# Output projection by halves of the tokens, with squares summed and weights cut on GpSimd

## The chip, the cores and the metric

The kernel runs on one core of a Trainium2 chip. The metric is the device time of one execution in microseconds (us). The kernel before took 2391.41 us, the median of 3 runs (2388.33 to 2393.7). A core has five engines that run their own instruction streams: TensorE (PE, matrix products; its weight loads are shown as PEld), VectorE (DVE), ScalarE (ACT), GpSimd (POOL) and SyncE (SP, which here issues the transfers).

## The reference, cut to what matters

Two blocks run one after the other, each with two layers, on 512 tokens of width 1024, in float32. The first block (three kinds of attention with gates) is not touched. A layer of the second block computes:

```python
h = rms_norm(x, norm1) * (1.0 + scale1) + shift1
proj = h @ w_in
y_pool = pool_mixer(u, pool_w, pool_scale)             # 512 wide
y_nsa = nsa_mixer(q, k, v, gates, ...)                 # 8 heads of 64, two softmax branches each
mix = concatenate([y_pool, y_nsa]) @ w_out
x = x + gate1 * mix
h2 = rms_norm(x, norm2) * (1.0 + scale2) + shift2      # needs the sum of squares over all 1024 of x
x = x + gate2 * (square(relu(h2 @ w_ff1)) @ w_ff2)
```

## The kernel before, in words

Everything is kept transposed: a tile has 128 of the 1024 channels as partitions and the 512 tokens as columns, so x is eight tiles `x(0)` to `x(7)`. Products are exact to float32 by splitting both sides into a high and a low part: `mm3` makes three products (high x high, high x low, low x high) for each pair of a 128x128 weight block and a token tile.

Weights come as units of 128x1024 (`unit`, line 430). SyncE loads a unit into `wraw`, ScalarE casts its high part into `wH` (line 452), VectorE subtracts to get the low part `wL` (line 453, here called a cut). In the second block there are three buffers of `wH` and of `wL`.

In the attention part of a layer (`main2`, line 1416) a main stream of projections is woven with side streams: `nsa` (line 1734) handles eight heads with two branches each, in two overlapping stages. The first stage makes scores on TensorE, masked rows on VectorE (line 710), exponentials on ScalarE (line 711), the reciprocal and the gate as `rsum` on VectorE (lines 1759 and 1760), and scales the probabilities, the first two of four token tiles on GpSimd (line 1764) and the others on VectorE (line 1766). The second stage transposes on TensorE, splits on ScalarE and VectorE (lines 419 and 420) and multiplies with the values. Other projections fill TensorE meanwhile: after the values (`values`, line 1485) come four units for the pooled channels, four units `o2` of the output projection for the pooled half of the mix, and two units `o2h` for heads 0 to 3 (two 128-row blocks of the mix).

The last part of the output projection takes heads 4 to 7 (`yn` blocks 2 and 3) with two units `("o2h", l, 1, 0)` and `("o2h", l, 1, 1)`, each for four output tiles. The first goes through `quad_unit` (line 550): each output over all 512 tokens in a PSUM bank of its own. The second goes through `in_halves` (line 478): first all four outputs for tokens 0 to 255, then all four for tokens 256 to 511. For each output that is done, `use2` (line 1521) adds it to x on VectorE (line 1507) and calls `stat_step` (line 647): ScalarE squares, VectorE adds the square to the running sum `ssq` (lines 657 and 661, shown as `keep`); the last output's square is not added but goes into the column sums as a second tile.

`turn` (line 500) carries this into the next projection. It drains the first half of the `in_halves` work, begins `stat_half` (line 663) of the first half, which it sets into the second half of the products after the yields numbered in `SLOTS = (1, 3)`, then drains the rest. A `stat_half` makes column sums on TensorE, the scale on VectorE (line 574), the power -1/2 on GpSimd (line 578), a broadcast by four short products on TensorE and a copy to `rbc` on ScalarE (line 678). Then `h2` (line 1341) makes the new h of that half, eight tiles, with two VectorE instructions (lines 1347 and 1349) and one of ScalarE (line 1348) each. The first three units of the next projection are done by halves too (`first`).

The order of instructions on each engine is set when the kernel is built: a planner simulates the program by program order, by priorities (`unit` asks for an early place) and by readiness; `issue_after` ties an instruction behind another. On the chip each engine runs its list in that order.

Of the kernel before, what the change touches and what calls it, by code (L numbers as in the profile page):

```python
# [11 lines left out]
AF = mybir.ActivationFunctionType  # L12
ALU = mybir.AluOpType
# [208 lines left out]
def fbits(ap):  # L222
    return ap.bitcast(F32)
# [53 lines left out]
class Builder:  # L277
    def __init__(self, ctx, tc, dram):
        self.tc = tc
        self.nc = tc.nc  # L280
        self.dram = dram
        self.sb = ctx.enter_context(tc.tile_pool(name="sb"))
        self.ps = ctx.enter_context(tc.tile_pool(name="ps", space=bass.MemoryType.PSUM))
        self.units = []
        self.uid = 0
        self.stream = "m"
        self.acc = "acc"
        self.block = "1"
        self.flags = set()
        self.squares = []  # L290
        self.queue = {}
        self.norms = 0
        self.background = iter(())
        self.bgrate = self.bgc = 0.0
# [135 lines left out]
    def unit(self, spec, whole=False):  # L430
        nc = self.nc
        i = len(self.units)
        self.units.append(spec)
        with self.tc.high_priority(offset=3000):
            raw = self.t((P, 1024), "wraw", 2)
            if i in self.queue:
                with self.tc.issue_after(self.queue[i].ins):
                    self.load = nc.sync.dma_start(raw, self.dram["wp"][i])
            else:
                self.load = nc.sync.dma_start(raw, self.dram["wp"][i])  # L440
            if whole:
                return raw
            if spec[0] == "gates":

                h = self.t((P, 8, 2, 32), "wH", 4, F32R)
                r = raw[:, 0:256].rearrange("p (k c) -> p k c", k=KT)
                self.cut_h = nc.scalar.copy(h[:, :, 0, :], r)
                self.cut = nc.vector.tensor_sub(h[:, :, 1, :], r, fbits(h[:, :, 0, :]))
                return h.rearrange("p k w c -> p (k w c)"), None
            h = self.t((P, 1024), "wH", 4, F32R)  # L450
            l = self.t((P, 1024), "wL", 4, F32R)
            self.cut_h = nc.scalar.copy(h, raw)  # L452
            self.cut = nc.vector.tensor_sub(l, raw, fbits(h))  # L453
        return h, l

    def after_unit(self, out, in_):
# [18 lines left out]
            self.products(ps, h, l, k, src.h(k), src.l(k), k == 0, k == KT - 1)  # L475
        return ps

    def in_halves(self, jobs, src, use, k0=0):


        made = []

        def emit(half):
            ts = slice(256 * half, 256 * half + 256)
            for i, (spec, outs) in enumerate(jobs):
                if half == 0:
                    made.append((self.unit(spec), [self.psum("acc") for _ in outs]))
                (h, l), ps = made[i]
                nk = KT // len(outs)
                for a, m in enumerate(outs):  # L490
                    for k in range(nk):
                        mm = self.products(ps[a][:, ts], h, l, a * nk + k, src.h(k0 + k, ts), src.l(k0 + k, ts), k == 0, k == nk - 1)
                        if k == nk - 1:
                            use(m, ps[a], ts)
                        if (a * nk + k) % 4 == 3:
                            yield mm

        return emit
# [147 lines left out]

    def stat_step(self, ssq, x, k, ts=None):
        nc = self.nc
        if k == 0:
            nc.scalar.activation(ssq, x, AF.Square)  # L650
        elif ts is not None:
            sq = self.tmp()[:, ts]
            nc.scalar.activation(sq, x[:, ts], AF.Square)
            if k == KT - 1:
                self.squares.append(sq)
            else:
                nc.vector.tensor_tensor(ssq[:, ts], ssq[:, ts], sq, ALU.add)
        else:
            sq = self.tmp()
            nc.scalar.activation(sq, x, AF.Square)  # L660
            nc.vector.tensor_tensor(ssq, ssq, sq, ALU.add)
# [689 lines left out]
    def block2(self, l, x, par, mt, ssq, emit, out):  # L1351

        nc = self.nc
        self.flags.clear()
        drain(self.background)
        us = {"u": [u_s("w_in_2", l, P * g) for g in range(4)], "k": [u_s("w_in_2", l, 1024 + 384 * s) for s in range(2)],
              "g": [("gates", l)]}
        us = [x for p in ORDER if p in us for x in us[p]][:NFIRST]
        hs, first = self.turn(emit, ssq, x, mt[:, 48:56], mt[:, 0:8], us)
        S = dict(l=l, par=dict(par, **self.params2_rest(l)), hs=hs, x=x, mt=mt, first=first)  # L1360

        def chain():
            yield from self.nsa_prep(S)
            yield from self.nsa(S)

        self.weave(self.main2(S), [["s", chain(), RATE2], ["c", self.compressed(S), RATEC], ["p", self.pool(S), RATEP]])
        us = [u_s("w_ff1_2", l, P * m) for m in range(NFIRST)]
        hs, first = self.turn(S["emit"], S["ssq"], x, mt[:, 56:64], mt[:, 24:32], us)

        f = {}  # L1370
        nxt = None
        if out is None:
            nxt = self.start_mod(l + 1)

        def ff1(q):
            f[q] = self.hl(KT)
            for m in range(KT):
                ps = first[m] if q == 0 and m < NFIRST else self.proj_s(u_s("w_ff1_2", l, 1024 * q + P * m), hs)
                r = self.tmp()
                nc.scalar.activation(r, ps, AF.Relu)  # L1380
                r2 = self.tmp()
                nc.vector.scalar_tensor_tensor(r2, ps, 0.0, r, ALU.max, ALU.mult)
                self.split(f[q].h(m), f[q].l(m), r2)
                if q > 0:
                    self.bg_step()

        s2 = self.new_ssq()

        def add(m, ps, ts=slice(None)):
            nc.vector.scalar_tensor_tensor(x(m)[:, ts], ps[:, ts], mt[:, 40 + m:41 + m], x(m)[:, ts], ALU.mult, ALU.add)  # L1390

        def add_last(m, ps, ts=None):
            add(m, ps, ts or slice(None))
            if out is None:
                self.stat_step(s2, x(m), m, ts)
            else:
                nc.sync.dma_start(out[:, m, ts or slice(None)], x(m)[:, ts or slice(None)])

        def ff2(q):
            use = add_last if q == 3 else add  # L1400
            n = KT - NLAST if q == 3 else KT
            for m in range(n):
                use(m, self.proj_s(("f2", l, q, m), f[q]))
                self.bg_step()
            return self.in_halves([(("f2", l, q, m), [m]) for m in range(n, KT)], f[q], use)

        ff1(0)
        ff1(1)
        ff2(0)
        ff1(2)  # L1410
        ff2(1)
        ff1(3)
        ff2(2)
        return s2, ff2(3), nxt

    def main2(self, S):
        nc, hs, l, x, mt = self.nc, S["hs"], S["l"], S["x"], S["mt"]
# [67 lines left out]
        def values():  # L1485

            ps = yield from self.proj_m([("kvs", l, i) for i in range(4)], hs)
            kw = S["kraw"] = self.b4((P, TT, 256))
            V = S["V"] = self.b4((P, 2, TT, P), F32R)
            W = S["W"] = self.b4((P, 2, TT, P), F32R)  # L1490
            for tt in range(TT):
                with self.soon():
                    nc.scalar.copy(kw[:, tt, :], ps[tt][:, 0:256])
                    src = ps[tt][:, 256:512].rearrange("p (b g d) -> p b g d", b=2, g=2)
                    for b, t in enumerate((V, W)):
                        self.split(t[:, :, tt, 0:64], t[:, :, tt, 64:128], src[:, b])
            self.flag("kv")
            self.rate["s"] = RATE3
            self.acc = "accn"

        parts = {"u": pooled, "k": windows, "g": gates, "q": queries, "w": hidden, "v": values}
        for p in ORDER:
# [11 lines left out]
        for mq in range(2):  # L1514
            for i, _ in enumerate(self.quad_unit(("o2h", l, 0, mq), S["yn"], 0, 4 * mq, use)):
                if i % 2:
                    yield
        yield "yn"
        ssq = S["ssq"] = self.new_ssq()

        def use2(m, ps, ts=None):
            use(m, ps, ts or slice(None))
            self.stat_step(ssq, x(m), m, ts)

        yield from self.quad_unit(("o2h", l, 1, 0), S["yn"], 2, 0, use2)
        S["emit"] = self.in_halves([(("o2h", l, 1, 1), [4, 5, 6, 7])], S["yn"], use2, 2)

    def pool(self, S):
        nc, l, par = self.nc, S["l"], S["par"]
# [372 lines left out]

NFIRST = 3
NLAST = 2
NLASTP = 2

SLOTS = (1, 3)

# [63 lines left out]
```

## Time and profile before

| | |
|---|---|
| median of 3 runs | 2391.41 us |
| the profiled execution, its own time | 2391.33 us |
| its span | 2389.5 us |
| TensorE (PE) busy | 2342.3 us, 98% |
| VectorE (DVE) busy | 1640.2 us, 69% |
| ScalarE (ACT) busy | 1048.7 us, 44% |
| GpSimd (POOL) busy | 264.3 us, 11% |
| chain that ended last | PE 93%, DVE 5%, ACT 1%, issue 1% |

The page divides the span into 40 slices of about 60 us; each digit is the busy share in tenths:

```profile
PE   8999999999999999999999989999999998999999
DVE  5679975567588987656579886666647988644342
POOL 0011010000001001000055310000005531000000
```

The second block begins at about slice 19. Its two layers show as the two places at which GpSimd is busy (slices 20 to 23 and 30 to 33). An engine's busy time says nothing of what bounds a stretch: which wait ends last there does. A busy TensorE counts products that are running, at either of the two levels of its clock (2.4 GHz, shown as 1.00, and 1.2 GHz, shown as 0.50; a value between them is a mean over the stretch).

### The profile page before, as it was taken

The numbers are of one execution on the slowest core, as the hardware profiler recorded it, in microseconds if no ns is written. First come the engines' busy times: TensorE is split into PE (matmuls) and PEld (weight loads), VectorE is DVE, ScalarE is ACT, GpSimd is POOL, SyncE is SP. The second block draws the span as 40 slices with busy tenths as digits, with TensorE's granted clock in tenths as the row PEclk, the third lists the DMA queues.
The fourth block names the chain that finished last, engine by engine and source line by source line (L and its number), as shares of the span: only waits on it lengthen the run. The fifth ranks groups of instructions, "written<-read, shape, count | busy, mean of one in ns | idle before, by whom it ended". The sixth has DMA issues, their size and how long they took to land.

```text
span 2389.5 us, 31476 instructions
## 1 busy us (share of the span) xinstructions
PE 2342.3 (98%) x11684; PEld 1973.3 (83%) x11684; DVE 1640.2 (69%) x3410; ACT 1048.7 (44%) x1930; POOL 264.3 (11%) x254
## 2 busy tenths in 40 slices
PE   8999999999999999999999989999999998999999
PEld 7888888888888888888888778888888876888888
DVE  5679975567588987656579886666647988644342
ACT  6455543434446554343246654332324665433231
POOL 0011010000001001000055310000005531000000
PEclk9999999999999999999999999999999999999999
DMA  5222222245543222225332013555523211223222
GB/s 173 88 80 71 80 80 97 82 156 205 182 159 115 71 80 80 97 88 172 126 102 80 27 37 104 193 194 194 193 97 105 68 35 37 80 94 100 98 93 84
DMA packets 87851, 256.62 MB, mean 107 GB/s; under 512 B 9745, under 2 KB 10769, under 8 KB 87697
## 3 DMA queue, kind: packets, MB, share of 16 engines
q1 hardware_dynamic: 87552, 254.45, 31.9%
q8 instruction: 92, 1.51, 0.3%
q14 instruction: 63, 0.51, 0.1%
q10 hardware_dynamic: 144, 0.15, 0.0%
HBM read 250.37 MB, written 4.19 MB: 107 GB/s over the span
## 4 chain that ended last, share of the span: by engine, by line
PE 93%; DVE 5%; ACT 1%; issue 1%; DMA 0%; POOL 0%; DVEq 0%; ACTq 0%; POOLq 0%
PE acc L406 78%; PE M L406 5%; PE accn L406 4%; PE S L406 3%; PE M L415 3%; DVE p L420 1%; DVE p L710 1%; DVE b L1507 1%; DVE wL L453 1%; ACT p L419 0%; DVE p L1766 0%; ACT p L711 0%; DVE tmp_s L1794 0%; DMA wraw<-wp_in 0%; ACT tmp_s L1792 0%
## 5 line engine op out<-in xcount | busy, mean ns | idle before, releaser
L406 PE MATMUL acc<-h,wH 128*128 128x512 f32 (+2 forms) x2944 | 872.6, 380 | 9.5 <-ACT h L423 7.3
L452 ACT CAST wH<-wraw 128x1024 fp32r<-128x1024 f32 x358 | 375.2, 1051 | 656.8 <-PE acc L406 400.0
L406 PEld LDWEIGHTS acc<-h,wH 128*128 128x128 f32 (+1 forms) x2944 | 537.4, 189 | 106.1 <-ACT h L423 7.3
L453 DVE TENSOR_TENSOR wL<-wraw,wH 128x1024 fp32r<-128x1024 f32 x358 | 437.5, 1223 | 164.9 <-ACT wH L452 156.9
L406 PE MATMUL acc<-h,wL 128*128 128x512 f32 (+1 forms) x1440 | 546.2, 380 | 0.0
L406 PE MATMUL acc<-b,wH 128*128 128x512 f32 (+1 forms) x1696 | 503.9, 374 | 0.0
L406 PEld LDWEIGHTS acc<-b,wH 128*128 128x128 f32 x1696 | 311.8, 189 | 56.3
L406 PEld LDWEIGHTS acc<-h,wL 128*128 128x128 f32 x1440 | 272.7, 190 | 49.6
L406 PE MATMUL acc<-wH,h 128*128 128x512 f32 (+1 forms) x1024 | 310.0, 380 | 0.0
L406 PE MATMUL acc<-b,wL 128*128 128x512 f32 (+1 forms) x784 | 291.5, 372 | 0.0
L406 PEld LDWEIGHTS acc<-wH,h 128*128 128x128 f32 x1024 | 187.2, 188 | 33.7
L406 PE MATMUL acc<-wL,h 128*128 128x512 f32 (+1 forms) x512 | 194.7, 380 | 0.0
L1390 DVE SCALAR_TENSOR_TENSOR b<-acc,keep,b 128x512 f32<-128x512 f32 (+1 forms) x68 | 48.9, 720 | 183.9 <-PE acc L406 183.5
L406 PEld LDWEIGHTS acc<-b,wL 128*128 128x128 f32 x784 | 147.9, 189 | 25.4
L711 ACT ACTIVATE p<-p,nb 128x128 f32<-128x128 f32 x192 | 107.9, 564 | 77.7 <-DVE nb L710 76.7
L1325 DVE SCALAR_TENSOR_TENSOR keep<-keep 128x512 f32<-128x512 f32 x192 | 126.0, 686 | 11.1 <-DMA keep<-w_mod_in 10.9
L578 POOL TENSOR_TENSOR sm_bs<-sm_as,keep 128x4 f32<-128x4 f32 (+1 forms) x48 | 65.7, 1376 | 413.4 <-DVE sm_as L574 374.1
L406 PEld LDWEIGHTS acc<-wL,h 128*128 128x128 f32 x512 | 96.5, 188 | 16.2
L406 PE MATMUL S<-b,b 128*128 128x128 f32 (+3 forms) x480 | 108.9, 338 | 0.1
L710 DVE CUSTOM_DVE_ANT_0 p<-S,keep 128x128 f32<-128x128 f32 x192 | 101.3, 542 | 4.9 <-PE S L406 3.6
L415 PE MATMUL M<-keep,p 128*128 128x128 f32 x608 | 97.4, 275 | 2.7 <-DVE tmp_s L1794 1.0
L406 PE MATMUL M<-p,b 128*128 128x256 f32 (+3 forms) x352 | 81.7, 323 | 10.3 <-DVE p L420 9.0
(294 smaller groups left out, 2898.8 us busy)
## 6 DMA issues: line engine op xcount, KB each, us to landing
wraw<-wp_in SPq DMA_DIRECT2D x364, 512.0 KB, 3.5
keep<-w_mod_in SPq DMA_DIRECT2D x192, 256.0 KB, 3.6
b<-x_in SPq DMA_DIRECT2D x8, 256.0 KB, 6.3
g<-x_in SPq DMA_DIRECT2D x8, 256.0 KB, 4.4
x_spill<-tmp_m SPq DMA_DIRECT2D x8, 256.0 KB, 3.9
g<-x_spill SPq DMA_DIRECT2D x8, 256.0 KB, 3.8
out<-b SPq DMA_DIRECT2D x6, 256.0 KB, 2.0
keep<-parq_in SPq DMA_DIRECT2D x2, 384.0 KB, 6.9
```

Source lines behind the costliest of these rows:

```text
L406: return self.nc.tensor.matmul(out, l, r, start=start, stop=stop)
L415: self.nc.tensor.transpose(out, in_, self.ident[:n, :n])
L420: return self.nc.vector.tensor_sub(l, src, fbits(h))
L452: self.cut_h = nc.scalar.copy(h, raw)
L453: self.cut = nc.vector.tensor_sub(l, raw, fbits(h))
L578: self.pow = nc.gpsimd.tensor_tensor(r[:p, :n], m[:p, :n], self.mhalf[:p, :n], ALU.pow)
L710: nc.vector.tensor_tensor_reduce(p, s, mask, nscale, 3e38, ALU.add, ALU.min, accum_out=nb)
L711: nc.scalar.activation(p, p, AF.Exp, bias=nb, scale=-1.0, accum_out=accum)
L1325: nc.vector.scalar_tensor_tensor(w, w, 1.0, crow[:, T * k:T * k + T], ALU.mult, ALU.mult, accum_out=ms[:, 2 * f + k:2 * f + k + 1])
L1390: nc.vector.scalar_tensor_tensor(x(m)[:, ts], ps[:, ts], mt[:, 40 + m:41 + m], x(m)[:, ts], ALU.mult, ALU.add)
L1507: nc.vector.scalar_tensor_tensor(x(m)[:, ts], ps[:, ts], mt[:, 16 + m:17 + m], x(m)[:, ts], ALU.mult, ALU.add)
```

## The change

Three things change in the second block, in both layers. The second part of the heads' output projection goes wholly through `in_halves`: all eight outputs for tokens 0 to 255, then all eight for tokens 256 to 511, two outputs sharing a PSUM bank (`shared`), so that all 96 products have 256 columns. The additions of squares in that part run on GpSimd (`adder`). And from the end of the value projection to the last heads the cuts of weight units run on GpSimd (`cutter`): ten units per layer, four for the pooled channels, four `o2`, two `o2h` for heads 0 to 3. The square of output 0 goes straight into its half of `ssq`.

```diff
     def unit(self, spec, whole=False):
...
-            self.cut = nc.vector.tensor_sub(l, raw, fbits(h))
+            self.cut = self.cutter.tensor_tensor(l, raw, fbits(h), ALU.subtract)
...
-    def in_halves(self, jobs, src, use, k0=0):
+    def in_halves(self, jobs, src, use, k0=0, shared=False):
...
-                    made.append((self.unit(spec), [self.psum("acc") for _ in outs]))
+                    made.append((self.unit(spec), None if shared else [self.psum("acc") for _ in outs]))
                 (h, l), ps = made[i]
                 nk = KT // len(outs)
                 for a, m in enumerate(outs):
+                    if shared:
+                        if m % 2 == 0:
+                            bank = self.psum("acc")
+                        o = bank[:, 256 * (m % 2):256 * (m % 2) + 256]
+                    else:
+                        o = ps[a][:, ts]
                     for k in range(nk):
-                        mm = self.products(ps[a][:, ts], h, l, a * nk + k, src.h(k0 + k, ts), src.l(k0 + k, ts), k == 0, k == nk - 1)
+                        mm = self.products(o, h, l, a * nk + k, src.h(k0 + k, ts), src.l(k0 + k, ts), k == 0, k == nk - 1)
                         if k == nk - 1:
-                            use(m, ps[a], ts)
+                            use(m, o if shared else ps[a], ts)
...
     def stat_step(self, ssq, x, k, ts=None):
         nc = self.nc
-        if k == 0:
+        if k == 0 and ts is not None:
+            nc.scalar.activation(ssq[:, ts], x[:, ts], AF.Square)
+        elif k == 0:
             nc.scalar.activation(ssq, x, AF.Square)
...
-                nc.vector.tensor_tensor(ssq[:, ts], ssq[:, ts], sq, ALU.add)
+                self.adder.tensor_tensor(ssq[:, ts], ssq[:, ts], sq, ALU.add)
...
         hs, first = self.turn(S["emit"], S["ssq"], x, mt[:, 56:64], mt[:, 24:32], us)
+        self.adder = nc.vector
...
             self.acc = "accn"
+            self.cutter = nc.gpsimd
...
+        self.cutter = nc.vector
         yield "yn"
         ssq = S["ssq"] = self.new_ssq()

-        def use2(m, ps, ts=None):
-            use(m, ps, ts or slice(None))
+        def use2(m, ps, ts):
+
+            nc.vector.scalar_tensor_tensor(x(m)[:, ts], ps, mt[:, 16 + m:17 + m], x(m)[:, ts], ALU.mult, ALU.add)
             self.stat_step(ssq, x(m), m, ts)

-        yield from self.quad_unit(("o2h", l, 1, 0), S["yn"], 2, 0, use2)
-        S["emit"] = self.in_halves([(("o2h", l, 1, 1), [4, 5, 6, 7])], S["yn"], use2, 2)
+        self.adder = nc.gpsimd
+        S["emit"] = self.in_halves([(("o2h", l, 1, mq), [4 * mq + i for i in range(4)]) for mq in range(2)],
+                                  S["yn"], use2, 2, True)
```

## Rows read from the trace of the kernel before

**Rows 1.** Busy time by stage: window, PE, PEld, DVE, ACT, POOL, PE clock, DMA.
```profile
1272.00:1410.00 138.00, 130.43 (x722) 107.85 (x721) 126.06 (x346) 89.73 (x236) 50.91 (x62) 1.00 0.12 39
1410.00:1420.00 10.00, 6.72 (x45) 5.35 (x42) 5.37 (x13) 4.16 (x10) 2.14 (x2) 1.00 0.16 53
1420.00:1430.10 10.10, 10.10 (x54) 8.94 (x54) 7.69 (x14) 3.67 (x6) 0.00 (x0) 0.83 0.01 2
1430.10:1440.70 10.60, 4.71 (x22) 4.41 (x20) 6.90 (x16) 4.12 (x11) 0.72 (x1) 0.67 0.31 99
1440.70:1450.00 9.30, 9.29 (x65) 9.29 (x66) 9.12 (x25) 5.74 (x14) 0.86 (x1) 0.82 0.00 0
1872.00:2003.50 131.50, 123.99 (x691) 102.53 (x690) 119.36 (x328) 87.43 (x229) 44.65 (x53) 1.00 0.11 37
```

**Rows 2.** Waits of PE, 1420 to 1441: us in total, times, longest.
```profile
PE M L406 <- DVE keep L657: 4.6, 1, 4.6
```

**Rows 3.** Timeline of DVE, 1422 to 1437: start, us, instruction.
```profile
1431.42 1.22 DVE L453 TENSOR_TENSOR wL<-wraw,wH 128x1024 fp32r<-128x1024 f32 x1
...
1433.27 2.88 DVE L657 TENSOR_TENSOR keep<-keep,tmp_m 128x256 f32<-128x256 f32 x6
```

**Rows 4.** Timeline of all engines, from the last heads to the next projection.
```profile
1419.98 1.12 PE L406 MATMUL accn<-b,wH 128*128 128x512 f32 x2 [2.04 <-ACT b L419]
...
1434.82 0.58 PE L406 MATMUL M<-keep 128*128 128x1 f32 x2 [4.59 <-DVE keep L657]
...
1437.13 0.72 POOL L578 TENSOR_TENSOR sm_bm<-sm_am,keep 128x2 f32<-128x2 f32 x1 [24.99 <-DVE sm_am L574]
...
1437.90 1.22 PE L406 MATMUL M<-keep,sm_bm 128*128 128x128 f32 x4 [1.22 <-POOL sm_bm L578]
...
1439.16 0.37 ACT L678 COPY keep<-M 128x256 f32<-128x256 f32 x1 [5.82 <-PE M L406]
...
1440.71 0.58 PE L406 MATMUL acc<-h,wH 128*128 128x256 f32 x1
```

**Rows 5.** Timeline of PE, 1455 to 1462, at full clock.
```profile
1456.00 0.40 PE L406 MATMUL acc<-h,wH 128*128 128x256 f32 x2
...
1456.36 0.40 PE L406 MATMUL acc<-h,wH 128*128 128x256 f32 x2
...
1460.66 0.63 PE L406 MATMUL acc<-h,wH 128*128 128x512 f32 x2
```

**Rows 6.** Groups of PE, 1420 to 1430.1: count, busy us, mean ns, idle before.
```profile
L406 PE MATMUL accn<-b,wH 128*128 128x512 f32 x12 | 4.9, 476 | 2.0 <-ACT b L419 2.0
```

**Rows 7.** Groups of DVE, 1420.5 to 1440.7.
```profile
L1507 DVE SCALAR_TENSOR_TENSOR b<-acc,keep,b 128x256 f32<-128x256 f32 x8 | 3.5, 477 | 0.0
...
L657 DVE TENSOR_TENSOR keep<-keep,tmp_m 128x256 f32<-128x256 f32 x6 | 2.5, 425 | 0.5
...
L661 DVE TENSOR_TENSOR keep<-keep,tmp_m 128x512 f32<-128x512 f32 x3 | 2.1, 686 | 0.0
```

**Rows 8.** Groups of ACT, 1420 to 1440.7.
```profile
L653 ACT ACTIVATE tmp_m<-b 128x256 f32<-128x256 f32 x8 | 2.6, 402 | 0.0
```

**Rows 9.** Groups of POOL, whole span, shapes kept apart.
```profile
L1546 POOL TENSOR_TENSOR tmp_p<-b 128x511 f32<-128x511 f32 x8 | 8.7, 1081 | 0.0
...
L1605 POOL TENSOR_TENSOR b<-keep 128x256 f32<-128x256 f32 x4 | 4.0, 998 | 0.0
```

**Rows 10.** Groups of DVE, 1272 to 1410.
```profile
L453 DVE TENSOR_TENSOR wL<-wraw,wH 128x1024 fp32r<-128x1024 f32 x11 | 13.4, 1217 | 0.0
```

**Rows 11.** Timeline of POOL, 1305 to 1310.
```profile
1306.05 0.19 POOL L1545 COPY tmp_p<-tmp_p 128x2 f32<-128x2 f32 x1
...
1307.29 1.11 POOL L1545 COPY tmp_p<-tmp_p 128x4 f32<-128x4 f32 x1
```

**Rows 12.** Timeline of DVE, 1306.5 to 1310.
```profile
1307.14 1.22 DVE L453 TENSOR_TENSOR wL<-wraw,wH 128x1024 fp32r<-128x1024 f32 x1
...
1308.94 1.00 DVE L420 TENSOR_TENSOR tmp_p<-tmp_p,tmp_p 128x512 fp32r<-128x512 f32 x1
```

More of the change, by code (lines that the diff above doesn't have):

```diff
@@ L284, in __init__ @@
         self.units = []
+        self.adder = self.nc.vector
+        self.cutter = self.nc.vector
         self.uid = 0
@@ L1904 @@
 NLAST = 2
-NLASTP = 2
 SLOTS = (1, 3)
```

## The prediction

> **What bounds the kernel now.** I read the page first: TensorE is busy for 98% of the span and the chain that ended last is TensorE for 93%, so a change pays only where TensorE stands still or runs at the lower clock. The row of slices shows two weak places, one in each layer of the second block, so I then read the busy time by stages [rows 1]. From the end of the value projection to the last heads (1272 to 1410 us) TensorE is busy 130.43 of 138 us and VectorE 126.06: both nearly full, with 7.6 us of idle TensorE. The same stretch of the second layer has 123.99 of 131.5, 7.5 us. The tail of the last two heads (1410 to 1420) leaves 3.3 us idle. Then comes the place that the change rebuilds, the turn from the output projection to the feed-forward part: in 1430.1 to 1440.7 TensorE shows 4.71 us in 10.6, nothing of it long matmuls, and the granted clock is 0.67.
>
> The waits of that stretch name one cause: 4.6 us for `keep` of line 657, the running sum of squares on VectorE [rows 2]; 1.2 us for GpSimd's power come behind it [rows 4]. In the second layer the same two waits are 4.6 and 1.1 us. Why VectorE is late is seen in its timeline [rows 3]: when TensorE has ended its products at 1430.1, VectorE still has a cut of weights before it (1431.42) and, from 1433.27 on, six additions of 256 columns. Only then can the chain of the norm start [rows 4]: column sums at 1434.82, power at 1437.13, broadcast at 1437.90, copy, scale and shift, and the first product of the next projection at 1440.71. From the high half of the last heads (1419.98) to there it is 20.7 us (20.6 in the second layer, from 2013.55 to 2034.17), while TensorE's products in it are worth about 9.
>
> Reason for the order: before, the first half of the tokens is not complete until the quad unit over all 512 tokens and its additions are done, and after the second half's four outputs no product is left to hide the norm of the first half. So the chain of the norm lies open in full.
>
> **The change part by part.** *Products by halves.* The 24 products of 512 columns become 48 of 256. In steady state three products of 256 columns start in 0.36 us, 0.12 each, and a pair of 512 lasts 0.63 us where a pair of 256 lasts 0.40 [rows 5], so that 256 more columns cost 0.115 and a product of 512 takes 0.235: 48 x 0.12 - 24 x 0.235 = 0.1 us more per layer. I count 0.2; rows of one steady stretch leave no more doubt than that, in either direction.
>
> *The turn.* Now the first half's eight outputs come first, then 48 products of the second half, with the norm's steps set among them (slots 1 and 3: after the 24th and after the 48th product). I build the time from 1419.98. Before that point 24 products of 256 columns (the part of the sum that the earlier heads feed) can run, as now 12 of 256 and 6 of 512 do: the trace has 54 products left after 1420 [rows 1], 18 of them of 512 (12 with high weights [rows 6] and half as many with low ones). Left are 24 + 48 = 72 x 0.12 = 8.6 us. The 54 now are worth 18 x 0.235 + 36 x 0.12 = 8.5 us and took 10.1 at a clock of 0.83, so I add 1.6 us for the low clock, all of it in the first half. First half ends at 1419.98 + 2.9 + 1.6 = 1424.5; the 24th product of the second half at 1427.4.
>
> Is the first half's sum there by 1427.4? VectorE adds the eight outputs to x, 0.41 us apart as now (477 ns each, overlapping) [rows 7]; with the first at about 1421 and TensorE's pace of 0.65 us per output while slow, the last is done at 1425. ScalarE squares each (402 ns [rows 8]): 1425.5. GpSimd's addition of 128x256 is not in the trace. Its two-input additions of 511 columns take 1081 ns in the mean, half of that is 0.54; other two-input instructions with 256 columns take 998 ns in the mean [rows 9]. I take 0.55, since the 511-column rows are the same plain form, and keep 1.0 as the upper end. Six in a row from 1422 end at 1425.7 (waiting for the last square), at the upper end at 1428. So the sum is there, or 0.6 us late. The low end, with additions that cost nothing, changes nothing here either, because ScalarE's last square then decides.
>
> Then: column sums of eight short matmuls, 1.9 us now at the low clock [rows 4], about 0.95 at full speed; the other 24 products to 1427.4 + 0.95 + 2.9 = 1431.3; the power (GpSimd, 0.72 us, VectorE 0.16) is hidden behind these; the broadcast, 1.22 us now, about 0.6 warm: 1431.9; and from the copy's start to the first product of the next projection 1.55 us as now (1439.16 to 1440.71) [rows 4]: 1433.5. Against 1440.7 that is **7.2 us less per layer**. What hides the chain is the second half's 48 products; if that cover were gone, the whole 7.2 would be back. VectorE's load in the turn falls by the additions, 6 x 0.42 + 3 x 0.69 = 4.6 us [rows 7], which go to a GpSimd that has nothing else there but two powers. What is late next: the weights of both quad units stay in use until the end of the second half, so the third buffer's cast and cut come at about 1430.5 to 1432.8, as now, and VectorE's cut (1.22 us) can push the first scaling by up to 1.2 us.
>
> *The clock.* After the gap it was still low at the start of the next projection (0.82 over 1440.7 to 1450 [rows 1]: 1.6 us lost). The new gap is about 1.6 us instead of ten; I leave this gain in the range, not in the sum, since the slow heads before it remain.
>
> *Cuts on GpSimd.* Ten cuts per layer leave VectorE; eight of the eleven in the stretch from 1272 are among them, 1.217 us each [rows 10], 9.8 us of VectorE there. On GpSimd a cut of 1024 columns is not shown; two of 511 columns are 2.16 us, my value; upper end 4.0 (four of 998 ns); lower end 1.2, as on VectorE, because no row shows it quicker. GpSimd has 50.9 us busy in 138 [rows 1]. Weights are cut a unit or more ahead of use, so 2 us instead of 1.2 reach TensorE late only if the cut queues behind a scaling of probabilities (line 1764) that itself waits for `rsum`.
> What comes back from the relief? TensorE's idle 7.5 us per layer is the most it can give. But the two engines get in each other's way: GpSimd's copy of four columns at 1307.29 took 1.11 us and ended with VectorE's cut of 1307.14 (the copy of two columns before: 0.19) [rows 11], and VectorE's addition of two SBUF tiles at 1308.94 took 1.00 us beside a GpSimd addition [rows 12], against 0.69 alone [rows 7]. The Trainium skill, "SBUF — State Buffer", section "Who interferes with whom", says that a VectorE instruction with two SBUF inputs and a GpSimd instruction that reads SBUF take turns on a shared port for the whole of an instruction. These two rows agree; by that rule alone ten cuts of 2.16 us, each stopping one such instruction for half its length, would hand back 10.8 of VectorE's 12.2 us per layer, the relief would be worth nothing, and the sum below would end at 2377.
> Most of VectorE's work here (rows, splits) reads PSUM, but `rsum` x gate before every scaling reads two SBUF tiles. From the 0.31 us lost beside one 1.03 us addition I scale to 0.65 per cut, 6.5 us back of 12.2. The remaining 5.7 shorten a stretch in which TensorE is full for 95%: I take a quarter, **1.5 us per layer**; bounds -4 to +5.
>
> *The square of output 0 by halves, the bank shared by two outputs:* ScalarE has 402 ns twice in place of one square of 512 columns, hidden by its idle time in the turn (4.12 us busy of 10.6 [rows 1]); eight banks pass one after another through the seven of their tag. Nothing; a bank that is not yet read would cost one wait of some 0.5 us, the time of one reading.
>
> **Sum.** 2 x (7.2 - 0.2 + 1.5) = 17 us. The profiled execution took 2391.33 us (span 2389.5 and 1.8 around it), the median is 2391.41: 2391.3 - 17 = **2374 us**. After the turn TensorE is full to the end of each layer, so that what is won there is not given back.
>
> **The rivals.** *A: VectorE's relief counts in full.* For it: VectorE is busy 91% of the stretch and TensorE's waits there are for its splits. Against: most of the wait is latency at the tail, which the cuts don't touch. With 5 instead of 1.5 us, the low clock gone at the start of the next projection (1.6) and an earlier start of the second half's products in the tail's 3.3 us idle (1), it is 2391.3 - 2 x 12.6, 2366.
> *B: the turn's gain is halved.* TensorE works in order, so the column sums at slot 1 hold up the rest of the second half if GpSimd's additions come late (1.0 us each and waits for VectorE's cuts), and the sums of the second half, placed ahead of the next products, stop it once more. For it: six dependent additions and the power share one queue. Against: two slack stages. With 3.5 per layer and no gain from the cuts: 2384.
> *C: slower, by GpSimd's queue in the heads' stretch.* The place is line 1764: a scaling of 128x128 and one of 256 per head and branch, on which the transposes wait. A cut in front of them delays them by up to 2.2 us, and by the shared port it stops `rsum` as well. If every one of the ten cuts lengthens the chain of heads by more than 0.7 us, the turn's 7.0 are gone; at 1.5 us each it is 2391.3 + 2 x (15 - 7.0), 2407; at 1.0 each 2397. For it: VectorE and the softmax chain hardly have slack. Against: heads are handled in two overlapping stages, and GpSimd is idle 87 us there.
> *D: the chain is reordered and nothing is won,* because the second half's norm now comes last and as late as the first half's did: 2390.
>
> **How the numbers follow.** Forecast 60% (2366 to 2382), A 12% (2360 to 2368), B 14% (2380 to 2388), C 10%, D 4%. Range 2363 to 2387: it leaves out a third of A, a little of B, and C and D. What a measurement here can tell from no change is 0.2%, 4.8 us; with that faster 0.84, within 0.2% 0.07 (D, the edge of B and of C), slower 0.09.
>
> **What would show it.** Right: in the turn no wait of TensorE for `keep`, a gap of 1.5 to 3 us before the first product of the next projection, 13 to 15 us from the high half to that product, additions of 0.5 to 0.7 us on GpSimd between squares. The heads' stretch within 3 us of 138 and 131.5, with cuts of 2 to 2.5 us on GpSimd. Wrong: a wait of TensorE for GpSimd's `keep` of over 2 us (B), POOL's scalings waiting in queue behind cuts and a heads' stretch of over 145 us (C), or cuts of 4 us, which the shared port would explain.

## The result and the profile after

The changed kernel took **2417.74 us** in the median of 5 runs (2414.71 to 2423.77) against 2391.41 (2388.01 to 2393.87, 5 runs) before: a ratio of 1.0114, 95% interval 1.0097 to 1.0131. It is slower by 1.1%; 2374 was forecast. The profiled execution was the longest of the five (2423.8 us, span 2422.0), so that the parts below add up to 32.5 us, while the medians lie 26.3 apart.

First the busy time by stages of the kernel before (columns as in [rows 1]), over two stages of each layer: the heads' stretch, from the layer's start (GpSimd's first memset) to the first product of the last part of the projection that needs the values of the last two heads (a few others run before it), and the turn, from there to the first product of the next projection.

```profile
1202.09:1419.98 217.89, 207.04 (x1162) 174.04 (x1160) 186.49 (x477) 127.77 (x311) 90.60 (x94) 0.99 0.19 61
1419.98:1440.71 20.73, 14.83 (x75) 13.38 (x75) 14.62 (x28) 7.81 (x17) 0.72 (x1) 0.75 0.16 51
1797.31:2013.55 216.24, 205.46 (x1161) 172.51 (x1159) 186.45 (x477) 127.77 (x311) 90.80 (x94) 1.00 0.18 59
2013.55:2034.17 20.62, 14.82 (x75) 13.43 (x75) 14.65 (x28) 8.13 (x17) 0.72 (x1) 0.76 0.16 52
```

The same four of the kernel after:

```profile
1201.07:1438.72 237.65, 217.29 (x1165) 179.60 (x1163) 188.87 (x467) 127.64 (x311) 112.07 (x104) 0.96 0.18 56
1438.72:1457.82 19.10, 14.54 (x95) 13.84 (x96) 13.93 (x26) 9.47 (x22) 10.06 (x13) 0.78 0.17 56
1815.24:2048.08 232.84, 212.99 (x1165) 176.42 (x1163) 186.65 (x467) 127.66 (x311) 111.99 (x104) 0.98 0.17 55
2048.08:2066.60 18.52, 13.24 (x96) 12.66 (x96) 12.90 (x25) 9.38 (x22) 10.23 (x13) 0.83 0.18 58
```

The heads' stretch grew by 19.8 and 16.6 us, the turn shrank by 1.6 and 2.1, and the rest of the span agrees within about a microsecond. About half of the growth is not standing still: TensorE's products, as many as before, were busy 10.3 and 7.5 us longer (217.29 for 207.04, 212.99 for 205.46), at a granted clock of 0.96 for 0.99 and 0.98 for 1.00. One more thing is to be seen: ten cuts less (467 instructions for 477) took nothing off VectorE's busy time, 188.87 us for 186.49. What the cuts had cost came back as longer instructions.

The turn's gain is partly the clock. A kernel with the old output projection and the old order on TensorE, ScalarE and VectorE (e7, below) has these two turns:

```profile
1416.52:1437.15 20.63, 14.83 (x74) 13.38 (x74) 14.61 (x28) 7.81 (x17) 0.72 (x1) 0.75 0.16 52
2011.40:2030.41 19.01, 13.27 (x74) 12.15 (x74) 14.47 (x28) 8.10 (x17) 0.72 (x1) 0.84 0.19 56
```

The same 74 products take 20.63 us at a granted clock of 0.75 and 19.01 at 0.84, and 1.56 of these 1.62 us are TensorE's busy time. Against the turn of like clock the changed kernel gains 1.5 us in the first layer (19.10 at 0.78) and only 0.5 in the second (18.52 at 0.83).

The groups on GpSimd that are new (columns as in [rows 9]):

```profile
L455 POOL TENSOR_TENSOR wL<-wraw,wH 128x1024 fp32r<-128x1024 f32 x20 | 48.3, 2414 | 58.9 <-ACT wH L454 58.9
...
L667 POOL TENSOR_TENSOR keep<-keep,tmp_m 128x256 f32<-128x256 f32 x24 | 17.9, 751 | 28.0 <-ACT tmp_m L663 26.7
```

A cut takes 2.41 us there (2.16 forecast), an addition of 128x256 0.75 (0.55). Both prices lie inside the bounds given for them (1.2 to 4.0 and up to 1.0).

### The profile page after: what moved, and what is told of

Read it like the earlier page. It is cut to its first block, busy times and chain, and to the rows that moved or that the text cites. A ratio compares the mean times of both kernels' runs of the same rounds, so it can differ in the third digit from the quotient of the medians.

```text
span 2422.0 us, 31602 instructions
## 1 busy us (share of the span) xinstructions
PE 2358.9 (97%) x11732; PEld 1983.1 (82%) x11732; DVE 1638.4 (68%) x3380; ACT 1050.3 (43%) x1938; POOL 325.8 (13%) x298
## 4 chain that ended last, share of the span: by engine, by line
PE 86%; DVE 8%; ACT 2%; POOL 2%; issue 2%; DMA 1%; POOLq 0%; ACTq 0%; DVEq 0%
PE acc L408 74%; PE M L408 5%; PE S L408 3%; PE accn L408 2%; PE M L417 2%; DVE p L422 1%; DVE p L720 1%; DMA wraw<-wp_in 1%; POOL sm_bs L586 1%; DVE wL L455 1%; ACT wH L454 0%; ACT p L421 0%; DVE p L1781 0%; DVE b L1519 0%; POOL tmp_s L1591 0%
## 5 line engine op out<-in xcount | busy, mean ns | idle before, releaser
L455 DVE TENSOR_TENSOR wL<-wraw,wH 128x1024 fp32r<-128x1024 f32 x338 | 414.0, 1225 | 167.3 <-ACT wH L454 162.1
L408 PE MATMUL acc<-b,wH 128*128 128x512 f32 (+1 forms) x1760 | 516.2, 371 | 5.0 <-ACT b L421 3.4
L408 PEld LDWEIGHTS acc<-b,wH 128*128 128x128 f32 x1760 | 321.5, 189 | 62.0 <-ACT b L421 3.8
L408 PE MATMUL acc<-b,wL 128*128 128x512 f32 (+1 forms) x816 | 301.0, 369 | 0.0
L408 PEld LDWEIGHTS acc<-b,wL 128*128 128x128 f32 x816 | 154.6, 189 | 25.0
```

Source lines behind the costliest of these rows:

```text
L408: return self.nc.tensor.matmul(out, l, r, start=start, stop=stop)
L455: self.cut = self.cutter.tensor_tensor(l, raw, fbits(h), ALU.subtract)
```

## The experiments

**The parts apart.** The cuts without the halves:

```diff
-            self.cut = nc.vector.tensor_sub(l, raw, fbits(h))
+            self.cut = self.cutter.tensor_tensor(l, raw, fbits(h), ALU.subtract)
...
             self.acc = "accn"
+            self.cutter = nc.gpsimd
...
+        self.cutter = nc.vector
         yield "yn"
```

> Kernel before, with only the ten cuts per layer moved to GpSimd. Theory 1 (the cuts on GpSimd lengthen the heads' stretch, which grew by 19.8 and 16.6 us in the two layers): 2418 to 2428 us, the heads' stretch as long as in the changed kernel, the turn as before (20.7 us). Rival (the products by halves and the additions on GpSimd make the planner place the heads' work worse): 2386 to 2396 us.

2420.82 us, ratio 1.0122 (1.0107 to 1.0137). The cuts alone make the whole loss.

The halves, with cuts and additions left on VectorE:

```diff
-            self.cutter = nc.gpsimd
...
-        self.adder = nc.gpsimd
```

> Changed kernel with cuts and additions back on VectorE; only the products by halves are left. Theory 1: heads' stretch as before (217.9 us from the layer's first GpSimd memset to the high half of the last heads), a turn of 17 to 20 us, 2384 to 2391 us. Rival (halves are at fault): 2410 us or more.

2392.05 us, 1.0002 (0.9993 to 1.0011): a microsecond above theory 1's range and far from the rival's. The halves are not at fault, but they win nothing that shows.

The halves with the additions on GpSimd (in this combination the seven `acc` banks don't fit beside the other PSUM tiles, so six):

```diff
-            self.cutter = nc.gpsimd
...
-        "acc2": 7,
+        "acc2": 6,
```

> Changed kernel with the cuts back on VectorE and the additions left on GpSimd; one PSUM bank fewer for the tag of the projections (six), since with seven the banks do not fit. Theory 1: heads' stretch as before, turn of 18.5 to 19.1 us as in the changed kernel, 2385 to 2392 us. Rival (halves or the additions are at fault): 2410 us or more.

2389.54 us, 0.9993 (0.9983 to 1.0003). In the profiles of the two the turn is 2.0 to 3.0 us shorter than before (0.7 to 1.9 against the turn of e7 with the like clock), not 7.2.

**What a cut on GpSimd costs.** Fewer of them, the changed kernel with the first four of each layer back on VectorE:

```diff
-            self.cutter = nc.gpsimd
...
         yield "yp"
+        self.cutter = nc.gpsimd
         for mp in range(4):
```

> Changed kernel with the four cuts of the pooled units back on VectorE; the six of the output projection stay on GpSimd. Theory 1a (the loss comes from cuts beside the serial chains of keys and compressed keys early in the stretch): 2390 to 2400 us. Theory 1b (each cut costs the same, 36 us over 20 cuts): 2391 - 4 + 0.6 x 36, 2405 to 2412 us.

2407.11 us, 1.0067 (1.0052 to 1.0082), where an even price per cut would put it. That reading turned out to be wrong (e9). What made me doubt it is that VectorE's instructions beside these twelve cuts were only some 6 us longer in all than the same instructions are in the kernel before, against some 22 us beside the twenty of the changed kernel, while both heads' stretches had grown (226.3 and 229.0 us). Laying the orders of issue side by side showed a second thing: the planner had put some 240 of TensorE's 11,424 products in other places than in e3 once the cuts counted as GpSimd's.

So the two had to be parted: the cuts with the old order, and the new order without the cuts. A kernel can plan twice and lay the first plan's order on the second:

```diff
+        if order:
+            for engine in ORDERED:     # PE, Activation, DVE, SP
+                names = [n for n in order[engine] if n in traced and str(traced[n].engine) == engine]
+                for a, c in zip(names, names[1:]):
+                    tc.add_manual_dep(traced[c], a, ..., reason="order")
...
+    _, order = trace(bacc.Bacc(...), relief=False)    # cuts on VectorE: plan only
+    units, _ = trace(nc, relief=True, order=order)    # cuts on GpSimd, that plan's order
```

GpSimd is not in `ORDERED`, since the cuts are new there: its own list is planned anew, and about ten of its 254 other instructions stand elsewhere in e5 than in the kernel before.

> The kernel before with the ten cuts of each layer on GpSimd (as in e1_cuts_only, 2420.8), but TensorE, ScalarE, VectorE and SyncE issue in exactly the order that they have in the kernel before; the planner put 200 products of TensorE elsewhere in e1 because the cuts count as GpSimd's there. Theory O (the loss is the new order of issue): the loss goes, 2380 to 2393, the relief of VectorE may even show. Theory L (the shared port: 22.5 us of VectorE's instructions stood still beside the cuts in e1): the cuts run as in e1, so 2412 to 2425. Theory Q (GpSimd works in order: a cut that waits for its `wH` holds the scalings behind it): as L, 2412 to 2425. In between (2396 to 2410) both parts count and their shares can be read off together with e6.

2405.29 us, 1.0055 (1.0042 to 1.0068). With `relief` the other way round:

> The counterpart of e5: the cuts stay on VectorE as in the kernel before (2391.0), but TensorE, ScalarE, VectorE and SyncE issue in exactly the order of e1_cuts_only. Theory O: 2412 to 2425 with no cut on GpSimd at all. Theories L and Q: 2387 to 2397, since neither the port nor GpSimd's queue is touched. If e5 and e6 both lose part, the losses should add up to about the 30 us of e1.

2408.50 us, 1.0074 (1.0060 to 1.0088). Neither theory holds alone: the new order by itself costs 17.7 us, without a single cut on GpSimd, and the cuts in the old order (of the other four engines) 14.5. Together 32.2, against 29.8 for e1.

The wait in GpSimd's queue, by itself:

```diff
+            nc.gpsimd.tensor_copy(self.t((P, 2), "dum", 1), fbits(h)[:, 0:2])
```

> The kernel before, cuts on VectorE, order of TensorE, ScalarE and VectorE the same to the last instruction; beside each of the ten units of a layer GpSimd copies two columns of `wH` into a scratch tile that nobody reads. GpSimd so waits in its queue for `wH` as it does for a cut, and then is busy for a fraction of a microsecond. Theory Q (the wait in the queue holds the scalings behind it): +10 to +30, 2401 to 2421. Theories L and O: 2389 to 2394.

2391.81 us, 1.0003 (0.9994 to 1.0012). Waiting for `wH` at the head of GpSimd's queue costs nothing that shows: the copies waited 50.2 us there in all. They took 0.28 us in the median, so this says nothing of a cut's 2.4 us of work in that queue.

The changed kernel with all its parts in the order of e3 (the edit of e5, six `acc` banks):

> The changed kernel with all its parts (halves, sums of squares on GpSimd, ten cuts on GpSimd; one buffer fewer for `acc`, 6 for 7, as in e3), TensorE, ScalarE, VectorE and SyncE in the order that e3_halves_pool_adds has (2389.5 with the cuts on VectorE). Theory O: 2378 to 2391, so the change as meant is no loss. Theories L and Q: 2408 to 2420, as e1 beside e3.

2403.54 us, 1.0052 (1.0040 to 1.0065): 14.2 us less than the changed kernel (which has seven `acc` banks), 14.0 more than e3, so between the theories.

**Where the 14 us are paid.** e5 and the kernel before issue the same products in the same order, so I set product against product. TensorE falls behind by 2.4 us in one step at 1262.6, by some 5.2 in the steps from 1282 to 1292, by 0.6 at 1323.5 and some 1.1 up to 1345.6, and gets about 1 us back at 1358.6; in the second layer by 2.1, 3.6, 0.5 and 1.7. Of the 5.2, some 1.7 are no wait but products at the lower clock behind the waits (0.66 over 1287.5 to 1292.5). In the timeline of e5 these are the places (GpSimd and VectorE; start, us, instruction):

```profile
1258.28 3.96 DVE L1677 CAST tmp_c<-tmp_c 64x64 fp32r<-64x64 f32 x1
1259.85 2.34 POOL L455 TENSOR_TENSOR wL<-wraw,wH 128x1024 fp32r<-128x1024 f32 x1
1275.29 2.50 POOL L455 TENSOR_TENSOR wL<-wraw,wH 128x1024 fp32r<-128x1024 f32 x1
1275.43 2.39 DVE L576 TENSOR_SCALAR sm_as<-sm_cs 128x4 f32<-128x4 f32 x1
1282.30 2.56 POOL L455 TENSOR_TENSOR wL<-wraw,wH 128x1024 fp32r<-128x1024 f32 x1
1282.54 2.47 DVE L1645 CAST p<-tmp_s 128x256 fp32r<-128x256 f32 x1
...
1285.98 1.25 POOL L1550 TENSOR_TENSOR tmp_p<-b 128x511 f32<-128x511 f32 x1
1287.18 1.26 POOL L1647 COPY p<-p 128x256 f32<-128x256 f32 x2
...
1297.37 2.39 POOL L455 TENSOR_TENSOR wL<-wraw,wH 128x1024 fp32r<-128x1024 f32 x1 [8.93 <-ACT wH L454]
1297.74 0.75 DVE L712 CUSTOM_DVE_ANT_0 p<-S,keep 128x512 f32<-128x512 f32 x1 [0.19 <-PE S L408]
...
1306.28 2.40 POOL L455 TENSOR_TENSOR wL<-wraw,wH 128x1024 fp32r<-128x1024 f32 x1
1306.71 0.68 DVE L1725 TENSOR_REDUCE cs<-tmp_c 128x16 f32<-128x512 f32 x1
```

and the waits of TensorE in e5's first heads' stretch (us in total, times, longest):

```profile
PE M L417 <- DVE tmp_c L1679: 2.4, 1, 2.4
...
PE M L417 <- POOL p L1647: 1.8, 1, 1.8
PE M L417 <- DVE p L1646: 1.3, 2, 0.9
```

Undisturbed, none of the three VectorE instructions before 1285 needs more than 0.3 us in this stretch of e5 (the cast of 1275.23 ran in 0.28, the 128x4 of 1273.96 in 0.16; the 64x64 shape's neighbours run in 0.22). Each stood until the cut beside it ended (the first behind two memsets of GpSimd as well): 1262.24 and 1262.19, 1277.82 and 1277.79, 1285.01 and 1284.86. This is not the loss of half an instruction, it is the loss of whole cuts, and in these first 85 us of a layer (windows, gates, pooling, mostly SBUF to SBUF in small steps) the next product waits for just that chain. Later VectorE works on scores in PSUM, and these pass: the masked row at 1297.74 begins beside a cut and takes 0.75 us, as it does alone. In all of e5, 29 instructions of VectorE with an operand in PSUM begin beside a cut, and none is more than 0.02 us longer than the median of its kind. A reduce of an SBUF tile passes too (last line).

One part of the price is GpSimd's own queue. The 1.8 us are a wait for its copy L1647, whose input, the cast, was there at 1285.01; but it began at 1287.18, behind L580 and L1550, which had themselves stood behind the cut. In the kernel before the planner had this copy ahead of the additions of the pooled part, which here come first:

```profile
1281.02 1.33 POOL L1643 COPY p<-p 128x256 f32<-128x256 f32 x1 [1.14 <-DVE p L1641]
...
1282.90 1.23 POOL L1546 TENSOR_TENSOR tmp_p<-b 128x511 f32<-128x511 f32 x1
```

The same wait of 1.8 us stands in the second layer, and in e8 and e10. What of it is the 2.4 us of work in GpSimd's queue, and what its new order, no run parts; the 2.4 us at the first cut are VectorE's standing alone.

If VectorE's small steps in SBUF are what counts, the first four cuts carry the whole price. The changed kernel in e3's order, cuts six only and four only:

```diff
         yield "yp"
+        self.cutter = nc.gpsimd if self.relief else nc.vector
         for mp in range(4):
```

> e8_after_old_order (2403.5 beside 2389.5 for e3, the same order of issue with all cuts on VectorE) with six of its ten cuts per layer on GpSimd, those of the units that are cut while heads are under way, and four back on VectorE. Theory P (what is left of the loss at the old order is paid where a VectorE instruction with its operands in SBUF stands behind a cut, and these are the first four cuts of a layer: in e5 TensorE fell behind by 2.4 us at the first and by 5.4 us from the third and fourth, by 0 to 0.8 us at each of the six later ones, and got some 0.8 back): 2388 to 2394. Theory E (an even price per cut, 14 us for 20 is 0.7 each): 2396 to 2400.

**2385.80 us** (2383.87 to 2386.83, 11 runs), **0.9974 (0.9965 to 0.9983)**: faster than both kernels, by more than theory P allowed (2388 to 2394).

```diff
             self.acc = "accn"
+            self.cutter = nc.gpsimd if self.relief else nc.vector
...
         yield "yp"
+        self.cutter = nc.vector
```

> The complement of e9: the first four cuts of each layer on GpSimd, the other six on VectorE, order of issue as in e3. Theory P: 2401 to 2406, as e8. Theory E: 8 cuts at 0.7 us, 2394 to 2397.

2403.83 us, 1.0059 (1.0046 to 1.0071): eight cuts cost what twenty cost. An even price is refuted. And e4 has the same twelve cuts as e9, which takes 21.3 us less: that is the order of issue together with one `acc` bank.

e9's four stages (columns as above):

```profile
1202.09:1418.53 216.44, 206.29 (x1162) 173.64 (x1160) 181.18 (x471) 127.41 (x311) 104.66 (x100) 0.99 0.19 61
1418.53:1437.20 18.67, 14.82 (x99) 14.15 (x99) 13.71 (x26) 9.59 (x22) 10.02 (x13) 0.81 0.17 57
1793.70:2011.10 217.40, 207.19 (x1161) 173.08 (x1159) 181.19 (x471) 127.56 (x311) 104.69 (x100) 0.99 0.18 58
2011.10:2029.08 17.98, 13.73 (x99) 13.09 (x99) 12.40 (x25) 8.76 (x21) 10.11 (x13) 0.86 0.19 60
```

The two turns give 2.1 and 2.6 us against the kernel before. Here the six cuts did come off VectorE, 5.3 of their 6 x 1.22 us in each layer (181.18 for 186.49), but the heads' stretches are 1.5 us shorter and 1.2 us longer than before: TensorE made next to nothing of it. The cuts without the halves should then do nothing:

> The kernel before, with its output projection as it was, in its own order of issue, and only the six later cuts of each layer on GpSimd. e9 (2385.8, halves as well) lies 4.8 us under the kernel before and about 3.7 under e3. Theory R (these cuts take 12 x 1.22 = 14.6 us from VectorE where hardly anything stands behind them, and part of that reaches TensorE): 2386 to 2389, so that the halves add the rest in e9. Rival (the gain of e9 needs the halves, the cuts by themselves do nothing): 2389.5 to 2392.

2389.86 us, 0.9996 (0.9988 to 1.0005; the edit of e9 and e5 in the kernel before). By themselves they do nothing that shows, so theory R falls. Nor do the halves with the additions by themselves (e3, 0.9993). Only both together are faster, and it is not the turn that tells e9 from e3: e3's turns are as long (18.76 and 18.09 us), its heads' stretches 1.0 us longer each, while all 11 runs of e9 lie below all 10 of e3. Why the two parts need each other stays open.

**The turn.** The column sums of the second half moved behind products of the next projection, in e3:

```diff
-        drain(self.stat_half(ssq, 1, self.squares))
+        stat = self.stat_half(ssq, 1, self.squares)
...
+        for i, mm in enumerate(first(0)):
+            if i in SLOTS2:            # (0, 2)
+                with self.tc.issue_after(mm.ins):
+                    next(stat)
+                next(stat, None)
+        drain(stat)
         self.h2(hs, x, a, shift, 1)
-        drain(first(0))
```

> e3_halves_pool_adds (2389.5: halves and sums of squares on GpSimd, cuts on VectorE) with one change in the turn: the column sums of the second half of the tokens are issued behind the first 12 products of the next projection and the broadcast behind 36, where in e3 they stand ahead of all of them. In e3 TensorE stood 3.0 us there for GpSimd's `keep` (its last additions end at 1435.82, first product of the next projection at 1437.61, its first operand's high part ready at 1435.93, the low part at 1436.50). Theory T (the turn's missing gain is this wait): the first product comes at 1436.0 to 1436.6, so 1.0 to 1.6 us less per layer, 2385.5 to 2388. Rival (the operand is as late as the sums, since VectorE's cut of 1432.87 and GpSimd's additions hold up the scaling): 2388.5 to 2391, the wait only changes its name.

2416.81 us, 1.0109 (1.0096 to 1.0123), outside both expectations. In the turn theory T's gain came: 16.9 and 16.3 us in the profile, 1.8 less than in e3 in each layer, though some of it is only moved, since TensorE now makes these sums behind the turn's end. The wait of 3.0 us for GpSimd's `keep` is gone; 2.6 us for ScalarE's `h` stand in its place, as the rival has it, but the sums no longer come between that operand and the first product. Yet some hundreds of TensorE's products stand elsewhere than in e3, and the heads' stretches, in which nothing was edited, take 226.0 and 223.9 us for 217.5 and 218.4; another 14 us went before the first of them and between the layers. That the new order eats more than the edit gives is how I read it; it was not parted from the edit here.

## Why the prediction was wrong

**The step that failed first: "From the 0.31 us lost beside one 1.03 us addition I scale to 0.65 per cut, 6.5 us back of 12.2. The remaining 5.7 shorten a stretch in which TensorE is full for 95%".** The addition of [rows 12] ran beside GpSimd for only a part of its length (GpSimd's addition ended 0.45 us after its start), and an average of it over all cuts says nothing of the place. Measured, in the old order: 2.2 us for a small instruction that meets the start of a cut, 0 for one that works on PSUM; four cuts per layer cost 14 us in two layers (a part of it by GpSimd's own queue, as shown above), the other six cost nothing. The trace of before had shown this, in a place that I did not read because no cut stood there (VectorE, then GpSimd):

```profile
1259.69 1.65 DVE L1673 CAST tmp_c<-tmp_c 64x64 fp32r<-64x64 f32 x1
```

```profile
1258.60 1.81 POOL L1679 MEMSET b<- 128x2048 f32 x1
1260.35 0.95 POOL L1689 MEMSET b<- 128x1024 f32 x1
```

A cast of 64 columns that lasts 1.65 us and ends at 1261.34, with the second memset (1261.30). It has one input, and GpSimd reads nothing: the rule as I had quoted it, two SBUF inputs against GpSimd's reads, does not cover it. The Trainium skill, "SBUF — State Buffer", section "Who interferes with whom", has more lines than the one I took: casts, copies and tensor-scalar instructions with their operands in SBUF can hold both ports too, and `tensor_reduce` never contends. The runs agree with each of these: 3.96 us for the cast, 2.39 for the 128x4 tensor-scalar, 0.68 for the reduce. By the whole rule, cast chains in the pooled part were the place to look.

**The step that was missing: the order of issue.** I counted what the edit adds to each engine and took the order around it as given. It is planned anew, over the whole program, when an instruction moves to another engine; that alone costs 17.7 us in e6, and with one `acc` bank more 14.2 in the changed kernel (against e8) and 21.3 in e4 (against e9). I can show where, not by which single swap. In e6, set beside the kernel before by VectorE's masked rows, 2.9 of the first heads' stretch's 7.2 us are lost before the first row, and 3.5 in the stretch whose windows are (kernel before, then e6):

```profile
1333.78:1365.40 31.62, 28.34 (x152) 23.59 (x153) 25.51 (x65) 16.74 (x43) 7.59 (x8) 1.00 0.15 51
```

```profile
1335.57:1370.67 35.10, 30.95 (x154) 25.32 (x155) 25.60 (x65) 16.87 (x42) 7.54 (x8) 0.95 0.16 46
```

The other windows between these rows differ by 0.8 and 0.0. It is the same work on every engine, 3.5 us longer, with a clock that dips (0.83 over 1337 to 1347, after a wait of 2.0 us for ScalarE; the kernel before waits 1.8 at that place and keeps 1.00).

**Rival C** named the right stretch and sign with 10%, and for 1.5 us per cut its 2407. Its mechanism was half right: VectorE did stop by the port. Of the queue part, the wait at its head costs nothing (e7), and cuts ahead of the scalings of line 1764 cost nothing either (e12); but early in the layer a copy of GpSimd's behind a cut held TensorE for 1.8 us. The price is not even over the cuts, and about half the loss has another cause.

**"First half's eight outputs come first, then 48 products of the second half": not in the plan.** In the changed kernel's order of issue the first output of every shared bank comes first, three of the second half among them, and only then the second ones; the column sums stand behind 69 of 75 products (in the second layer behind all 75), not behind the 24th of the second half. The cover that the sum relied on was gone. The prediction had put the shared bank at "nothing", apart from a wait of 0.5 us; the order goes just by these banks, though no run changes that alone. The turn's timeline in the first layer:

```profile
1444.76 3.52 POOL L667 TENSOR_TENSOR keep<-keep,tmp_m 128x256 f32<-128x256 f32 x5 [13.56 <-ACT tmp_m L663]
...
1447.22 1.05 ACT L454 CAST wH<-wraw 128x1024 fp32r<-128x1024 f32 x1 [1.10 <-PE acc L408]
...
1448.46 1.22 DVE L455 TENSOR_TENSOR wL<-wraw,wH 128x1024 fp32r<-128x1024 f32 x1
1448.73 2.76 POOL L667 TENSOR_TENSOR keep<-keep,tmp_m 128x256 f32<-128x256 f32 x3 [0.45 <-ACT tmp_m L663]
...
1450.22 0.38 PE L408 MATMUL M<-keep 128*128 128x1 f32 x2 [1.49 <-POOL keep L667]
...
1452.32 3.72 POOL L667 TENSOR_TENSOR keep<-keep,tmp_m 128x256 f32<-128x256 f32 x4
...
1453.09 1.67 DVE L455 TENSOR_TENSOR wL<-wraw,wH 128x1024 fp32r<-128x1024 f32 x1 [0.48 <-ACT wH L454]
1453.40 0.37 ACT L688 COPY keep<-M 128x256 f32<-128x256 f32 x1
...
1454.69 1.64 DVE L1357 SCALAR_TENSOR_TENSOR tmp_m<-b,keep 128x256 f32<-128x256 f32 x2
...
1456.10 0.59 PE L408 MATMUL M<-keep 128*128 128x1 f32 x2 [2.76 <-ACT h L1358]
```

GpSimd's additions go by output number; the first one needs an odd output, which is late, so they start at 1444.76 (forecast, moved to this start: 1440.7), pause while ScalarE has a weight cast ahead of the next square, and end at about 1450. TensorE waits 1.49 us (4.6 in [rows 2]). Then the cut that I allowed 1.2 us for takes 1.67 beside GpSimd's additions, two scalings take 1.64 where 0.87 is usual, and the second half's sums hold TensorE until 1457.82, as rival B had it. That last one is worth at most 1.8 us per layer (e11). So B's mechanisms are all there, and the turn's gain is 1.6 and 2.1 instead of 7.2, at like clock 1.5 and 0.5.

**The three terms together.** Of the 43 us between forecast and result the turn makes some 12 (14.0 us forecast for the turn and the halves, 1.5 won in e3), the cuts in the old order 17 (3 us forecast to be won, 14.0 lost in e8), and the new order 14. One sum of the prediction is wrong by itself: rival A's terms (7.0, 5, 1.6 and 1) add up to 14.6 us per layer, not 12.6, so to 2362, still inside A's range.

**What held:** TensorE's share for halves (75 to 96 instructions in the turn, its busy time no longer than before), the cut's and the addition's durations within their bounds, and that GpSimd's queue in the turn is the term to watch. The relief, sized at 1.5 us per layer with bounds of -4 and +5, is about nothing for the six later cuts (e12) and -7 per layer for the first four (e10 against e3: 14.3 us in two layers).

## What to carry to other kernels

When work moves to GpSimd, go through VectorE's instructions at the places where it will run: those with operands in SBUF (casts and small scalar steps too) may stand until it ends, those on PSUM pass; move it only beside the latter. Look also at what GpSimd itself does there that others wait for, since its own steps queue behind the new work. When a planner sets the order, an edit has two effects, and they must be measured apart: lay the old order on the new program before judging the edit, since here a program with twelve moved cuts was 0.67% slower than the kernel before in the planner's order and, with one `acc` bank fewer, 0.26% faster in the old one. Before counting on cover, read in the issue order that the covering work really stands behind the step.

## What the runs showed of the hardware

A short VectorE instruction stands as long as a long one: 16 bytes per partition (128x4) took 2.39 us beside a cut, 1024 bytes (128x256) 2.47. GpSimd suffers as well: its additions of 128x256 take 0.70 us in a row (3.52 for five) and 0.92 (2.76 for three) with VectorE's cut of 1448.46 beside them. A wait at the head of GpSimd's queue, which I had feared most, cost nothing (e7, 1.0003). And the same turn took 20.63 us at a granted clock of 0.75 and 19.01 at 0.84 (e7, its two layers), a difference as large as the gain that is looked for: a stage of one profile is to be compared at like clock.
